# Projection pairs two at a time in program order, and the start of attention inside the last two

## The chip, the core and the metric

The kernel runs on one core of a Trainium2 chip. The metric is device time in microseconds for one launch: 2081.24 us before, the median of 3 runs (2080.03 to 2082.38).

## The reference

One layer of a streaming encoder on a 1024 x 1024 float32 input: a feed-forward block, a combined projection, a gated convolution beside differential attention, an output projection, a second feed-forward block, a final norm.

```python
h = x + 0.5 * swiglu(rms_norm(x, norm_ffn1), ffn1_gate, ffn1_up, ffn1_down)
u = rms_norm(h, norm_mix)
xc, bg, cg, q, k, v, g_conv, g_attn = split(u @ w_in)      # 1024 x 5120
y_conv = (bg * causal_conv3(cg * xc)) @ w_conv_out
q, k = rope(q), rope(k)                                    # 8 half heads of 64
o = softmax(q1 k1^T / 8, chunk mask) @ v - lam * softmax(q2 k2^T / 8, chunk mask) @ v
y_attn = ((1 - lam_init) * rms_norm(o)) @ w_attn_out
h = h + (sigmoid(g_conv + b) * y_conv + sigmoid(g_attn + b) * y_attn) @ w_o
h = h + 0.5 * swiglu(rms_norm(h, norm_ffn2), ...)
out = rms_norm(h, norm_final)
```

## The kernel before

Stages follow one another on one core: feed-forward 1, the projection with `w_in`, attention, the two branches' output projections, `w_o`, feed-forward 2. Each fp32 operand of a large product is split into a high and a low part of a narrower type (`split`, L245: a cast on ScalarE, ACT, for the high part, a subtraction on VectorE, DVE, for the low one), and a product is three matmuls (`mm3`, L264).

The projection has 20 blocks of weights of 1 MB. Sixteen are multiplied before attention and four (the second gate, `g_attn`) during it, as filling for the tensor engine (PE). A block, called a **pair**, is two column blocks of `w_in`: for example `c,0` holds `cg` and `xc` of a quarter of the convolution, `k,0` the two rotary halves of four half heads. Pairs 0 and 1 run as plain jobs; pairs 2 to 15 run by a seven-product scheme in the order `ORDER = (2, 1, 7, 6, 4, 5, 3)` (`pair_jobs`, L279). So a pair is seven **jobs**, and a job is 12 matmuls of 128x512 (L267).

A job has a `prep`, which sums quarters of the weight block on DVE (L243), casts the sum on ACT (L248, tiles `A` and `F`) and subtracts on DVE (L243), and a `run`: the 12 matmuls, then the eviction of the PSUM bank into one of ten `C` buffers, by an ACT copy where the target is new (L308) and a DVE add where it isn't (L310). The seven jobs of a pair share three accumulating chains: job 2 alone, jobs 1, 6, 5, 3, and jobs 7, 4. Job 6 goes on in the bank of job 1 and so must come after that bank has been read out; likewise 5 after 6, 3 after 5, and 4 after 7. `submit` (L214) keeps four jobs ahead: `prep` of job n+4 stands in the program ahead of `run` of job n.

When a pair's results are done, a function for its kind runs at once: `rope_done` (L800; six DVE products and sums and eight stores for each half), `v_done` (L825; a store), `conv_done` (L831; two DVE multiply-adds and an ACT scaling for each half, stored in `zd`), `bg_done` (L856; loads `zd` back, multiplies by the gate, stores `yd`). The pairs go k0, q0, v0, k1, q1, v1, c0, c1, b0, c2, c3, b1 (`PAIRS`, L882) after the first gate's four.

From `k.flush()` (L1260) backward, a scheduler of the framework orders the instructions of each engine by estimates of its own. From L1262 on, `manual_schedule` holds PE, DVE, ACT and GpSimd (POOL) to the order of the program; the queue of DMA issues on SyncE (SP) is scheduled throughout. [...]

In `run`, after the flush, the first steps of `filling` load and split block 16 of `w_in`; `attend` begins with `head(0)` (L901: loads of keys and values of head 0, casts L918, POOL subtractions L919, eight transposes of the values L929 and their splits), between whose steps four filling steps run (`FIRST`, L1241; six matmuls of L1159 each), then `load_q` (L934), then 16 **units** of attention. A score is L955, with a mask matmul L957. Each unit has filling steps of its own; what is left of the filling when the units are done runs after them.

## Time and profile before

| what | us or share |
|---|---|
| median of 3 runs | 2081.24 |
| profiled execution: its own time | 2082.11 |
| profiled execution: span | 2080.3 |
| PE busy | 1981.0 (95%) |
| DVE busy | 1402.0 (67%) |
| ACT busy | 935.1 (45%) |
| POOL busy | 136.8 (7%) |
| pairs 2 to 15, first matmul at 714.15 to last eviction's start at 1013.55 | 299.40 |
| from there to the first score at 1027.88 | 14.33 |
| unit 0 of attention, to 1038.54 | 10.66 |

The stretches are cut by the starts of instructions in the timeline. A matmul's end is modelled, so the pitch of successive jobs tells more than the duration of a row.

### The profile page before, as it was taken

Reading aid. Unit: us, or ns where it says so; the run is one execution under the profiler, and the core shown is the slowest. Engines: PE = TensorE matmul, PEld = TensorE weight load, DVE = VectorE, ACT = ScalarE, POOL = GpSimd, SP = SyncE. Lnnn points to the kernel's source line nnn. Section 1 sums busy time; section 2 is a strip of 40 time slices with the busy share of each in tenths; the row PEclk is TensorE's granted clock in tenths of the full one; section 3 lists DMA queues with packets and bytes.
Section 4 is the critical chain, followed back from the end, with each engine's and each line's share of the span. In section 5 each row is a group of like instructions: output and inputs, shape, how many; then the busy total and the mean of one; then the engine's idle time right before and its main releaser. Section 6 shows DMA issues by size and latency. Waiting matters only on the chain.

```text
span 2080.3 us, 24145 instructions
## 1 busy us (share of the span) xinstructions
PE 1981.0 (95%) x8808; PEld 1624.7 (78%) x8808; DVE 1402.0 (67%) x2166; ACT 935.1 (45%) x1684; POOL 136.8 (7%) x123
## 2 busy tenths in 40 slices
PE   9799999999999999999799997999999999999997
PEld 8588888888877877777578775877788888888885
DVE  8965665676866856656376737798865665666874
ACT  7433333353464633233366656456433333353362
POOL 0000000000000000000244445000000000000000
PEclk9899999999999999999899998999999999999998
DMA  5223223264543423312333344423223223274441
GB/s 213 84 109 113 95 102 117 81 236 159 194 157 111 152 98 100 126 57 71 119 105 122 97 148 144 190 81 132 97 102 121 86 101 112 82 264 152 150 154 59
DMA packets 81208, 259.70 MB, mean 125 GB/s; under 512 B 10048, under 2 KB 16320, under 8 KB 63936
## 3 DMA queue, kind: packets, MB, share of 16 engines
q1 hardware_dynamic: 81088, 258.15, 34.8%
q8 instruction: 69, 1.13, 0.2%
q14 instruction: 51, 0.42, 0.1%
HBM read 183.14 MB, written 74.97 MB: 124 GB/s over the span
## 4 chain that ended last, share of the span: by engine, by line
PE 81%; DVE 10%; ACT 3%; issue 2%; POOL 1%; DMA 1%; SPq 0%; DVEq 0%; ACTq 0%; POOLq 0%
PE sc L267 37%; PE at L267 16%; PE ps L267 9%; PE ot L267 8%; DVE Q L243 3%; PE ps L1159 2%; DVE A L243 1%; DVE C L243 1%; DVE F L243 1%; PE ps L1221 1%; PE sc L955 1%; PE sc L339 1%; PE sc L338 1%; PE sc L337 1%; PE sc L1221 1%
## 5 line engine op out<-in xcount | busy, mean ns | idle before, releaser
L267 PE MATMUL sc<-Q,A 128*128 128x512 f32 x1968 | 473.5, 390 | 2.4 <-ACT C L308 2.4
L267 PEld LDWEIGHTS sc<-Q,A 128*128 128x128 f32 x1968 | 369.7, 188 | 81.3 <-ACT C L308 3.2
L267 PE MATMUL sc<-Q,F 128*128 128x512 f32 x1548 | 382.1, 396 | 29.5 <-ACT Q L248 11.4
L267 PEld LDWEIGHTS sc<-Q,F 128*128 128x128 f32 x1548 | 294.6, 191 | 96.9 <-ACT Q L248 12.9
L243 DVE TENSOR_TENSOR F<-Q,F 128x512 fp32r<-128x512 f32 (+1 forms) x307 | 211.8, 696 | 170.1 <-ACT F L248 169.7
L248 ACT CAST F<-Q 128x512 fp32r<-128x512 f32 (+1 forms) x315 | 190.0, 612 | 256.5 <-PE sc L267 88.1
L243 DVE TENSOR_TENSOR Q<-Q,Q 128x512 fp32r<-128x512 f32 (+4 forms) x334 | 278.7, 887 | 33.6 <-ACT Q L248 26.8
L248 ACT CAST A<-Q 128x512 fp32r<-128x512 f32 (+1 forms) x299 | 180.3, 611 | 268.0 <-PE sc L267 159.1
L243 DVE TENSOR_TENSOR A<-Q,A 128x512 fp32r<-128x512 f32 (+1 forms) x299 | 202.0, 678 | 130.2 <-ACT A L248 129.3
L267 PE MATMUL at<-Q,F 128*128 128x512 f32 x1128 | 279.4, 393 | 10.1 <-ACT C L308 9.2
L267 PEld LDWEIGHTS at<-Q,F 128*128 128x128 f32 x1128 | 213.0, 189 | 57.3 <-ACT C L308 10.9
L248 ACT CAST Q<-Q 128x512 fp32r<-128x512 f32 (+1 forms) x214 | 153.1, 759 | 87.0 <-DVE Q L243 31.1
L243 DVE TENSOR_TENSOR C<-C,C 128x512 f32<-128x512 f32 x236 | 161.5, 688 | 16.6 <-DMA C<-zd 5.0
L243 DVE TENSOR_TENSOR Q<-Q 128x512 f32<-128x512 f32 x216 | 148.3, 690 | 3.7
L267 PE MATMUL ps<-Q,A 128*128 128x512 f32 x498 | 124.2, 390 | 0.0
L308 ACT COPY C<-sc 128x512 f32<-128x512 f32 x88 | 51.4, 588 | 156.5 <-PE sc L267 155.4
L267 PE MATMUL ot<-Q,A 128*128 128x512 f32 x450 | 112.8, 392 | 0.9 <-DVE Q L398 0.9
L267 PEld LDWEIGHTS ps<-Q,A 128*128 128x128 f32 x498 | 93.6, 188 | 19.6 <-issue 0.3
L1159 PE MATMUL ps<-Q,F 128*128 128x512 f32 x384 | 105.9, 412 | 3.1 <-ACT C L1165 3.1
L267 PE MATMUL at<-Q,A 128*128 128x512 f32 x444 | 107.6, 389 | 0.8 <-DVE C L310 0.8
L310 DVE TENSOR_TENSOR C<-C,sc 128x512 f32<-128x512 f32 x81 | 55.6, 687 | 75.3 <-ACT C L308 35.1
L267 PEld LDWEIGHTS ot<-Q,A 128*128 128x128 f32 x450 | 85.3, 190 | 19.0 <-issue 1.3
(218 smaller groups left out, 2190.6 us busy)
## 6 DMA issues: line engine op xcount, KB each, us to landing
Q<-in_ffn_gate SPq DMA_DIRECT2D x21, 1024.0 KB, 5.8
Q<-in_ffn_up SPq DMA_DIRECT2D x21, 1024.0 KB, 4.8
Q<-in_w_in SPq DMA_DIRECT2D x20, 1024.0 KB, 5.4
g1d<-C SPq DMA_DIRECT2D x77, 256.0 KB, 2.0
g2d<-C SPq DMA_DIRECT2D x77, 256.0 KB, 2.0
Q<-in_ffn_down SPq DMA_DIRECT2D x16, 1024.0 KB, 6.5
Q<-g1d SPq DMA_DIRECT2D x14, 1024.0 KB, 6.3
Q<-g2d SPq DMA_DIRECT2D x14, 1024.0 KB, 5.8
```

Source lines behind the costliest of these rows:

```text
L243: e.tensor_tensor(out, a, b, op)
L248: self.nc.scalar.copy(hi, src)
L267: mm = lambda *x, **kw: self.nc.tensor.matmul(*x, skip_group_check=True, **kw)
L308: nc.scalar.copy(C[o, t], ps)
L310: nc.vector.tensor_tensor(C[o, t], C[o, t], ps, ALU.add)
L337: mm(ps, a[:, 0, q], hi[:, q], start=n == q == 0, stop=False)
L338: mm(ps, a[:, 0, q], lo[:, q], start=False, stop=False)
L339: mm(ps, a[:, 1, q], hi[:, q], start=False, stop=n == 1 and q == 3)
L955: nc.tensor.matmul(sc[:, a : a + w], qs[:, hl, s, qb * P : (qb + 1) * P], kst[:, s, a : a + w], start=hl == 0, stop=hl == 1 and a + w < n)
L1159: nc.tensor.matmul(ps, a[kk][:, x, q], y[:, q], start=c == 0, stop=c == 23)
L1221: nc.tensor.matmul(ps, a[:, x, kk], b[:, y, kk % 2], start=c == 0, stop=c == 11)
```

## The change

The pairs 2 to 15 are taken two at a time by `two`, a **couple**: jobs of the two pairs alternate in the program. The order of pairs becomes b0 with k0, b1 with q0, c0 with v0, c1 with k1, c2 with q1, c3 with v1, after the gate's couple (2, 3). Couple (2, 3) is still ordered by the scheduler; the six couples from pair 4 on stand inside `manual_schedule`, so the written order is their order. The rope and convolution work is put into a queue `slow`, from which `aside` takes a step or two after each job. The gate `b` now comes before the convolution: it is stored in `bd`, and the convolution loads it and multiplies. During the last couple the nine steps of `head(0)` are appended to `slow`. After the last job is submitted, `load_q(0, 0)` and the first filling step (load and split of block 16) are issued, then the last jobs run. The four `FIRST` filling steps are no longer run there.

```diff
+    def aside(self, n=None):
+        for _ in range(min(len(self.slow), n or (2 if len(self.slow) > 3 else 1))):
+            self.slow.popleft()()
...
                 if LAST[o, t] == i:
                     done(o, t, C[o, t])
+                self.aside()
...
-        self.zd = [d(f"zd{j}", [P, SEQ]) for j in range(4)]
+        self.bd = [[d(f"bd{a}{t}", [P, 2, TH]) for t in range(2)] for a in range(2)]
...
+            def products():
+                tt(b, x2, sin, ALU.mult)
+                tt(d, x1, sin, ALU.mult)
+                tt(x1, x1, cos, ALU.mult)
+
+            def sums():
+                tt(x2, x2, cos, ALU.mult)
+                tt(x1, x1, b, ALU.subtract)
+                tt(x2, x2, d, ALU.add)
+                for hh, x in ((0, x1), (1, x2)):
+                    for c4 in range(4):
+                        nc.sync.dma_start(dst[c4, 32 * hh : 32 * hh + 32, t * TH : (t + 1) * TH], x[32 * c4 : 32 * c4 + 32, :])
+
+            k.slow.extend((products, sums))
...
+            def half(th):
+                zc, z, b = X[0, th], Z[th], k.C()
+                nc.sync.dma_start(b, self.bd[j // 2][th][:, j % 2])
                 nc.scalar.mul(zc, z[:, 2:], w(2))
...
-                nc.sync.dma_start(self.zd[j][:, th * TH : (th + 1) * TH], zc)
+
+                def gated():
+                    k.tt(zc, zc, b, ALU.mult)
+                    nc.sync.dma_start(self.yd[j // 2][th][:, j % 2], zc)
+
+                k.slow.appendleft(gated)
+
+            k.slow.extend((lambda: half(0), lambda: half(1)))
...
-             + [("k", 0), ("q", 0), ("v", 0), ("k", 1), ("q", 1), ("v", 1)]
-             + [("c", 0), ("c", 1), ("b", 0), ("c", 2), ("c", 3), ("b", 1)]
+             + [("b", 0), ("k", 0), ("b", 1), ("q", 0), ("c", 0), ("v", 0)]
+             + [("c", 1), ("k", 1), ("c", 2), ("q", 1), ("c", 3), ("v", 1)]
...
-            tp = k.ps("at")
+            tp = k.ps("at") if h else k.psd()
...
-        for i, _ in enumerate(self.head(0)):
-            if i in self.FIRST:
-                fill()
-        for _ in self.load_q(*units[0]):
-            pass
+        for _ in self.first:
+            fill()
...
-                if n == 2 and len(raws) < ns:
+                if n in (2, 4) and len(raws) < ns:
                     raws.append(k.load_raw(io["w_in"][len(raws)]))
...
-        for idx in range(2, ns):
-            project(k.pair_jobs(raws[idx], B, self.done(idx)))
-        k.flush()
+        doubles = lambda idx: project(k.two(*(k.pair_jobs(raws[i], B, self.done(i)) for i in (idx, idx + 1))))
+        doubles(2)
         ET = mybir.EngineType
         with k.tc.manual_schedule(engines={ET.PE, ET.DVE, ET.Activation, ET.Pool}):
+            self.first = self.head(0)
+            for idx in range(4, ns, 2):
+                if idx == 4:
+                    self.cs = k.t("Q", [P, 2, SEQ])
+                    nc.sync.dma_start(self.cs, io["rope"])
+                if idx == ns - 2:
+                    k.slow.extend([lambda: next(self.first, None)] * 9)
+                doubles(idx)
...
+            queries = self.load_q(0, 0)
+            next(queries)
             next(fill)
+            k.step()
+            for _ in queries:
+                pass
+            k.flush()
+            while k.slow:
+                k.aside()
```

Two places show it in the queues of the engines. A name such as `C_757_6426` is a buffer's tag and a running number.

**Place 1**, ACT where one pair ends and the next begins, before: `at_739` is here the bank of v1's last job, `at_751` and `ps_756` are banks of the first jobs of the next pair, c0.

```order
L248 CAST A_758_6428<-Q_746_6334 128x512
L308 COPY C_749_6371<-at_739_6267 128x512
L308 COPY C_752_6390<-at_751_6377 128x512
L308 COPY C_757_6426<-ps_756_6413 128x512
L248 CAST A_763_6466<-Q_746_6334 128x512
```

The same engine after, within the couple b1, q0; the four banks hold jobs of the two pairs in turn.

```order
L314 COPY C_694_5872<-at_693_5859 128x512
L254 CAST A_695_5874<-Q_649_5493 128x512
L314 COPY C_697_5890<-sc_696_5877 128x512
L254 CAST F_698_5893<-Q_644_5453 128x512
L314 COPY C_699_5908<-at_689_5822 128x512
L254 CAST A_700_5911<-Q_649_5493 128x512
L314 COPY C_701_5926<-sc_691_5842 128x512
```

Before, three copies stand in a row, and the first of them reads a bank that PE writes later than the other two; after, copies and casts alternate in the order in which PE fills the banks.

**Place 2**, DVE at the end of the last pair, before: `at_836` and `sc_839` are banks of b1's jobs. The low part of block 16's first slice (`F_854`) stands nine rows ahead of this piece.

```order
L310 TENSOR_TENSOR C_834_7081<-C_834_7081,at_836_7087 128x512
L850 SCALAR_TENSOR_TENSOR C_830_7051<-C_831_7053,cst_1_85,C_830_7051 128x512
L243 TENSOR_TENSOR C_834_7081<-C_834_7081,C_837_7101 128x512
L851 SCALAR_TENSOR_TENSOR C_830_7051<-C_831_7053,cst_1_85,C_830_7051 128x512
L310 TENSOR_TENSOR C_841_7135<-C_841_7135,sc_839_7108 128x512
L243 TENSOR_TENSOR C_841_7135<-C_841_7135,C_842_7150 128x512
L310 TENSOR_TENSOR C_840_7121<-C_840_7121,at_836_7087 128x512
```

After, at the end of the last couple (c3, v1): `C_846` takes the eviction of v1's job 4 from `sc_830`; `C_840` and `C_842` take those of the two jobs 5, from `at_834` and `sc_837`; `Q_859` is block 16, `Q_856` an operand of the filling.

```order
L316 TENSOR_TENSOR C_846_7119<-C_846_7119,sc_830_6968 128x512
L256 CAST Q_857_7166<-Q_856_7164 128x512
L249 TENSOR_TENSOR Q_858_7167<-Q_856_7164,Q_857_7166 128x512 x2
L256 CAST Q_857_7166<-Q_856_7164 128x512
L249 TENSOR_TENSOR F_860_7178<-Q_859_7176,F_860_7178 128x512
L316 TENSOR_TENSOR C_840_7052<-C_840_7052,at_834_6995 128x512
L316 TENSOR_TENSOR C_842_7072<-C_842_7072,sc_837_7019 128x512
```

And the DMA queue, SP, there, before and after: the load of block 16 and its neighbours.

```order
L863 DMA yd00_3219<-C_792_6723 128x512
L276 DMA Q_853_7207<-in_w_in 128x2048
L863 DMA yd01_3220<-C_790_6706 128x512
L861 DMA C_800_6787<-zd0_3235 128x512
L863 DMA yd01_3220<-C_799_6785 128x512
```

```order
L956 DMA C_854_7160<-qkq0_3211 64x2x256 x2
L840 DMA vd3_3218<-C_846_7119 128x512
L282 DMA Q_859_7176<-in_w_in 128x2048
L840 DMA vd3_3218<-C_842_7072 128x512
L863 DMA C_864_7231<-bd10_3237 128x512
```

The low part of block 16's first slice now stands on DVE ahead of the evictions of both jobs 5, and the load of block 16 stands on SP behind the store of `C_846`, which waits for the first of these rows; before, it stood among the stores of `yd0`.

## Rows read from the trace of the kernel before

**Rows 1.** The page: busy time per engine; shares of the chain that ended last.

```profile
PE 1981.0 (95%) x8808; PEld 1624.7 (78%) x8808; DVE 1402.0 (67%) x2166; ACT 935.1 (45%) x1684; POOL 136.8 (7%) x123
...
PE 81%; DVE 10%; ACT 3%; issue 2%; POOL 1%; DMA 1%; SPq 0%; DVEq 0%; ACTq 0%; POOLq 0%
```

**Rows 2.** Windows: stretch, length, busy us per engine (count), PE's granted clock, DMA share, GB/s.

```profile
150.00:250.00 100.00, 100.00 (x443) 82.83 (x442) 59.62 (x91) 37.68 (x66) 0.00 (x0) 1.00 0.30 114
714.15:1013.55 299.40, 280.03 (x1195) 226.12 (x1193) 181.90 (x285) 99.22 (x175) 4.58 (x7) 0.98 0.30 99
1013.55:1027.88 14.33, 4.53 (x14) 3.46 (x15) 2.01 (x3) 4.89 (x9) 4.99 (x5) 0.64 0.56 168
1027.88:1038.54 10.66, 9.79 (x36) 8.10 (x37) 3.29 (x9) 6.03 (x17) 4.28 (x4) 0.69 0.43 135
1242.40:1277.70 35.30, 34.21 (x135) 24.78 (x134) 22.10 (x20) 21.63 (x37) 25.57 (x18) 1.00 0.39 119
```

**Rows 3.** Window of the filling line L1159 alone: PE and PEld only.

```profile
714.15:1013.55 299.40, 4.57 (x18) 3.38 (x18) 0.98 0.30 99
```

**Rows 4.** Timeline of PE: start, us, instructions, idle before and its releaser.

```profile
809.46 4.50 PE L267 MATMUL at<-Q,F 128*128 128x512 f32 x12 [2.59 <-ACT C L308]
...
816.51 2.88 PE L267 MATMUL ps<-Q,F 128*128 128x512 f32 x12
819.23 2.88 PE L267 MATMUL sc<-Q,A 128*128 128x512 f32 x12
822.89 3.01 PE L267 MATMUL sc<-Q,F 128*128 128x512 f32 x12 [0.78 <-DVE C L310]
...
895.46 3.01 PE L267 MATMUL ps<-Q,F 128*128 128x512 f32 x12 [1.43 <-ACT C L308]
```

**Rows 5.** Timeline of ACT at the boundary of place 1.

```profile
893.84 1.07 ACT L308 COPY C<-at 128x512 f32<-128x512 f32 x2 [10.03 <-PE at L267]
894.80 0.60 ACT L308 COPY C<-ps 128x512 f32<-128x512 f32 x1
```

**Rows 6.** Timeline of PE from the last projection job to the first score.

```profile
1010.53 3.02 PE L267 MATMUL at<-Q,A 128*128 128x512 f32 x12 [0.78 <-DVE C L310]
1022.07 1.11 PE L929 MATMUL at<-ident,C 128*128 128x128 f32 x4 [8.53 <-DMA C<-vd]
1025.54 1.05 PE L929 MATMUL at<-ident,C 128*128 128x128 f32 x4
1027.88 0.45 PE L955 MATMUL sc<-Q,A 128*128 128x128 f32 x1 [1.29 <-ACT A L943]
```

**Rows 7.** Timeline of DVE in the pairs.

```profile
777.42 1.29 DVE L243 TENSOR_TENSOR C<-C,C 128x512 f32<-128x512 f32 x2
...
939.38 0.74 DVE L851 SCALAR_TENSOR_TENSOR C<-C,cst,C 128x512 f32<-128x512 f32 x1
...
947.32 2.38 DVE L243 TENSOR_TENSOR Q<-Q,Q 128x512 fp32r<-128x512 f32 x2
...
1015.14 0.69 DVE L243 TENSOR_TENSOR C<-C,C 128x512 f32<-128x512 f32 x1 [3.94 <-DMA C<-zd]
```

**Rows 8.** Timeline of POOL beside it.

```profile
946.89 1.66 POOL L243 TENSOR_TENSOR Q<-Q,Q 128x512 fp32r<-128x512 f32 x1 [50.23 <-DVE A L243]
```

**Rows 9.** Timeline of SP: DMA issues.

```profile
951.42 0.33 SPq L276 DMA_DIRECT2D Q<-in_w_in  x1
...
1011.60 0.43 SPq L861 DMA_DIRECT2D C<-zd  x1
```

**Rows 10.** DMA issues between 700 and 1060: count, KB each, median us to landing.

```profile
Q<-in_w_in SPq DMA_DIRECT2D x14, 1024.0 KB, 5.3
```

**Rows 11.** Timeline of PE after a long pause, behind attention.

```profile
1286.42 1.22 PE L1221 MATMUL sc<-Q,F 128*128 128x512 f32 x2 [8.66 <-ACT F L248]
...
1289.94 4.39 PE L1221 MATMUL sc<-Q,F 128*128 128x512 f32 x10 [1.05 <-DVE F L243]
1294.17 2.45 PE L1221 MATMUL ps<-Q,A 128*128 128x512 f32 x10
```

More of the change, by code (lines that the diff above doesn't have):

```diff
@@ L177, in __init__ @@
         self.bg = deque()
+        self.slow = deque()
         self.rot = self.na = 0
@@ L811, in done @@
             tt = k.tt
-            tt(b, x2, sin, ALU.mult)
-            tt(d, x1, sin, ALU.mult)
-            tt(x1, x1, cos, ALU.mult)
-            tt(x2, x2, cos, ALU.mult)
-            tt(x1, x1, b, ALU.subtract)
-            tt(x2, x2, d, ALU.add)
-            dst = self.qk[which, p]
-            for hh, x in ((0, x1), (1, x2)):
-                for c4 in range(4):
-                    nc.sync.dma_start(dst[c4, 32 * hh : 32 * hh + 32, t * TH : (t + 1) * TH], x[32 * c4 : 32 * c4 + 32, :])
+            dst = self.qk[which, p]
+            def products():
[10 more added lines that the diff above has]
+            k.slow.extend((products, sums))
         return done
@@ L846, in done @@
             w = lambda a: k.cst[:, C_CW + 3 * j + a : C_CW + 3 * j + a + 1]
-            for th in range(2):
-                zc, z = X[0, th], Z[th]
+            def half(th):
+                zc, z, b = X[0, th], Z[th], k.C()
+                nc.sync.dma_start(b, self.bd[j // 2][th][:, j % 2])
                 nc.scalar.mul(zc, z[:, 2:], w(2))
@@ L859, in done @@
         def done(o, t, c):
-            zc = k.C()
-            nc.sync.dma_start(zc, self.zd[2 * jp + o][:, t * TH : (t + 1) * TH])
-            k.tt(c, c, zc, ALU.mult)
-            nc.sync.dma_start(self.yd[jp][t][:, o, :], c)
+            nc.sync.dma_start(self.bd[jp][t][:, o, :], c)
         return done
@@ L888, in loads @@
         k = self.k
-        r = [k.load_raw(k.io["w_in"][0]), k.load_raw(k.io["w_in"][1])]
-        self.cs = k.t("Q", [P, 2, SEQ])
-        k.nc.sync.dma_start(self.cs, k.io["rope"])
-        return r
+        return [k.load_raw(k.io["w_in"][0]), k.load_raw(k.io["w_in"][1])]
     def done(self, idx):
@@ L1240 @@
     NPLAIN = 4
-    FIRST = (4, 5, 6, 7)
     def run(self, raws, f, load_h, done, pre):
```

## The prediction

> **What bounds the kernel now.** I read the page first: PE is busy 95% of the span and carries 81% of the chain that ended last, DVE is busy 67% and is 10% of that chain [rows 1]. So time is to be had only where PE stands still or runs at a lower clock, and the windows say where. In feed-forward 1, where two pairs of products alternate in the program, PE is busy the whole of 100 us at a granted clock of 1.00, with DVE busy 60% [rows 2]. In the projection's pairs it isn't: 299.40 us hold 280.03 busy; then come 14.33 us with 4.53 busy at a clock of 0.64, and unit 0 with 0.69 [rows 2].
>
> The timeline shows the pauses. Two jobs start 2.72 us apart (816.51 and 819.23), and that pitch is the price of 12 matmuls when nothing is missing, 0.227 us each [rows 4]. A pair has two kinds of pauses. At its boundary PE waits 1.4 to 2.6 us for an ACT copy; behind the longer ones 12 matmuls take 4.50 us where they otherwise show 2.88, since the clock has fallen. And its last job waits 0.78 us for a DVE eviction, because the chain's bank can't be written on before it has been read [rows 4]. ACT shows the first kind as a queue: at place 1 two copies in a row begin at 893.84, after 10.03 us of waiting for PE's last job of the old pair; the copy of `ps`, behind them, begins at 894.80, and PE, which needs that bank, goes on at 895.46 [rows 5, 4]. The bank of `ps` had been filled long before. So the first kind comes from the order on ACT, the second from a chain with nothing beside it.
>
> The stretch after the pairs is another thing: the last job begins at 1010.53, and PE next works at 1022.07, having waited 8.53 us for the values' load; the first score is at 1027.88 [rows 6].
>
> **The change part by part.**
>
> *The pairs.* 14 pairs x 7 jobs x 2.72 = 266.6 us is the dense time of the work from 714.15 on; its 98 x 12 = 1176 matmuls remain. Of the 299.40 us, 18 are filling matmuls, 18 x 0.227 = 4.1 [rows 3], and 299.4 - 266.6 - 4.1 = 28.7 are pauses and low clock. With two pairs alternating, a job of the other pair (2.72) lies between two jobs of one chain, which covers the 0.78; the ACT copies stand in the order in which the banks fill, which ends the 1.4 to 2.6. What can be late next is DVE. It is busy 181.9 us here [rows 2]; over 266.6 that is 68%, against 60% in feed-forward 1, where two alternating pairs leave no pause. The margin is 32% of a couple's 38.1 us, some 12 us, but the order is now the written one: `aside` puts three rope products (0.65 each from the pair at 777.42, 1.9 together [rows 7]) or two convolution steps (0.74 each) between an eviction and the next job's operands. An eviction has 2.72 us from the end of its job to the start of the next of its chain: its own 0.65 and 1.9 fit, with 0.2 left. I take 0.3 us for each of the seven couples, 2 in all; the bounds are 0 and 8, the latter one pause of about 1.2 per couple.
>
> *Head 0.* The 14.33 us from 1013.55 to the first score go. Their loads, casts, and POOL subtractions come to lie beside the last couple's matmuls. Eight transposes stay on PE's path, 1.11 + 1.05 as shown; by then the values' load may be just late. I take 1.7, bounds 0.8 to 3. Six filling matmuls in that stretch move away too.
>
> *The load of block 16.* Here the change adds a wait. On SP it stands behind the store of `C_846`, which waits for the DVE eviction of v1's job 4; on DVE the low part of its first slice stands ahead of the evictions of both jobs 5, and PE's last two jobs wait for those. From the end of job 4: eviction 0.65, the store's issue 0.43 [rows 9], the load 5.3 [rows 10], a cast 0.6, the low part 0.65, the eviction of job 5 0.65, and some 0.5 for hand-overs (0.06 between the end of the copy at 895.40 and PE at 895.46, several times over): 8.8. In that time PE has two jobs, 5.4. So the third stands still for 3.4 us; bounds 1.5 (a load without neighbours) and 8 (a load that shares the DMA engines with the last rope stores and head 0's loads). Before, the load was issued at 951.42, far from any end [rows 9], and cost nothing. Then the clock: after a pause of 2.59 twelve matmuls take 1.6 more, after one of 8.66 the next fourteen take (1286.42 to 1294.17) 7.75 instead of 3.2, of which 1.05 is a pause [rows 4, 11]. For 3.4 I take 2.0, nearer the first; bounds 0 and 4.
>
> Up to the first score: 266.6 + 2.0 + 1.7 + 3.4 + 2.0 = 275.7 in place of 299.4 + 14.3 = 313.7, a gain of 38.0.
>
> *Unit 0.* It took 10.66 us at a clock of 0.69 with 36 matmuls, 9.79 busy [rows 2]; at full clock some 3 us less. But its first maxima stand on DVE behind the last convolution steps, six operations of 0.65 to 0.74 (4.2 us), which nothing covers but the first score. I take 0, bounds -3 and +3.
>
> *The filling.* Four steps of six matmuls, 24, no longer run ahead of attention; the units have their own, so 24 remain for its end. There PE is busy 34.21 of 35.30 at a clock of 1.00 [rows 2], so they cost 24 x 0.227 = 5.4; the lower bound is 0, if the pauses behind that stretch (8.66 [rows 11]) take them up.
>
> *POOL.* Eight subtractions now fall in the last couple. At 946.89 one took 1.66 beside two DVE subtractions of 2.38, which take 1.29 together without it [rows 7, 8]: 1.1 of DVE's time. With DVE's margin of 12 us even eight such (8.8) fit; I take 0, and the bound is one of them in front of an eviction, 1.1. [...]
>
> The sum: -38.0 + 0 + 5.4 = -32.6. The profiled execution took 2082.1, 0.9 over the median of 2081.2 and well inside what three runs spread, so 2082.1 - 32.6 = **2049.5**.
>
> **The rivals.**
>
> (a) *Slower: the written order on DVE and ACT.* Both execute in order, and a scheduler's order is replaced by one that knows no durations. The place is DVE within each of the six written couples: a convolution product that waits for the load of the gate, as DVE waited 3.94 us at 1015.14 for `zd` [rows 7], holds every operand and eviction behind it. Two such waits in a couple are 8 us, and the clock falls after each (1.6). The decision point is 32.6 / 6 = 5.4 us lost per couple; at two waits with their clock, 11 x 6 = 67 less 2 already counted, the time would be 2114, at 8 us per couple 2096. For it: every `C` buffer is needed, 10 for about 16 tiles a couple, so that loads are issued late. Against: the gate's product is a step of its own, taken a job or more after its load was issued, and the load issued at 1011.60 served the product at 1015.14, 3.5 us or 1.3 jobs later [rows 7, 9]. [...]
>
> (b) *Faster, but with half of it eaten.* The same mechanism in two or three couples only, or buffers late for the operands: 10 to 27 us back, 2066 to 2077.
>
> (c) *No change.* Pauses of the first kind return in full as DVE pauses: 28.7 of the 38.0 back, with the filling's 5.4: 2078 to 2085.
>
> (d) *The larger gain.* Block 16 lands in time (-5.4), the filling disappears in later pauses (-5.4) and unit 0 gains its clock (-3): 2036, with DVE's 2 also 2034; beyond that there is nothing to take.
>
> That it doesn't do what it says is excluded: the queues of place 1 show the new order, and head 0's steps stand among the last couple's jobs.
>
> **How the numbers follow.** The forecast with its bounds covers 2034 (all at the lower end) to 2066 (stalls in order +6, block 16 +4.6, clock +2, unit 0 +3, rounded): 0.76. Case (b) 0.10, (c) within 0.2% 0.04, (a) 0.07, below 2034 0.03. 0.2%, 4 us, is about what a measurement of this kernel can tell from no change. That makes faster 0.89, same 0.04, slower 0.07. The range holds the forecast and the nearer end of (b): 2034 to 2068.
>
> **What would show it.** In the profile after: from the first job of couple (2, 3) to the last projection job 266 to 275 us; no ACT copy ahead of which ACT waits 10 us; the load of block 16 issued within some 10 us of the last job, one pause of 2 to 5 us on PE behind it, released by DVE, and a clock below 1 after it; the first score near 990; more L1159 matmuls or later work after the last unit. I am wrong if PE shows pauses in every couple with DVE as releaser (a), if the pause at block 16 is missing or over 8, or if the gain up to the first score is there and lost again in the units.

## The result, and the profile after

The changed kernel takes 2047.38 us (2045.84 to 2049.32, 4 runs) against 2080.95 for the kernel before in the same comparison: a ratio of 0.9839, 95% interval 0.9822 to 0.9856. The forecast was 2049.5, a gain of 32.6 in the profiled execution; that gained 35.5 (2082.11 to 2046.62). The total fits better than its parts do: too little was charged up to the first score, and stretches that were put at nothing made up for most of it.

| stretch | before | after | gain | forecast gain |
|---|---|---|---|---|
| up to the first matmul of pair 2 | 714.15 | 713.33 | 0.8 | 0 |
| from there to the first score | 313.73 | 281.30 | 32.4 | 38.0 |
| unit 0 | 10.66 | 9.54 | 1.1 | 0 |
| unit 1 to the long pause | 239.23 | 242.60 | -3.4 | -5.4 |
| the long pause | 8.65 | 8.76 | -0.1 | 0 |
| from its end to the end of the span | 793.88 | 788.97 | 4.9 | 0 |

The windows of the profile after, cut at the same events (stretch, length, busy us of PE, PEld, DVE, ACT and POOL with their counts, granted clock, DMA share, GB/s), answer to [rows 2]:

```profile
713.33:947.73 234.40, 231.93 (x1021) 191.16 (x1020) 151.47 (x237) 86.55 (x155) 5.21 (x7) 1.00 0.31 105
947.73:994.63 46.90, 40.96 (x164) 33.55 (x165) 31.39 (x48) 14.98 (x27) 5.82 (x6) 0.89 0.37 116
994.63:1004.17 9.54, 7.15 (x38) 5.79 (x36) 5.14 (x12) 5.75 (x16) 1.52 (x2) 1.00 0.34 110
1004.17:1246.77 242.60, 228.24 (x1221) 187.34 (x1219) 151.85 (x281) 152.84 (x373) 116.80 (x97) 1.00 0.37 117
1255.53:2044.50 788.97, 764.11 (x3332) 627.40 (x3332) 551.92 (x826) 343.40 (x570) 1.29 (x1) 0.99 0.35 129
```

The same two last stretches of the kernel before, from its own windows:

```profile
1038.54:1277.77 239.23, 224.42 (x1197) 184.99 (x1195) 148.53 (x276) 149.89 (x367) 115.88 (x96) 0.99 0.36 113
1286.42:2080.30 793.88, 767.28 (x3332) 628.90 (x3332) 553.96 (x828) 343.64 (x571) 0.92 (x1) 0.98 0.35 129
```

The pairs are dense: 85 jobs at 2.72 are 231.2, and PE goes from 713.33 to 945.38 (947.73 less a wait of 2.35), 232.05, at a clock of 1.00. What is left of pauses stands at the end of the last couple. The timeline of PE there (start, us, instructions, idle before and its releaser; an L273 is the L267 of before, L945 the transposes, L971 a score):

```profile
947.73 0.98 PE L945 MATMUL sc<-ident,C 128*128 128x128 f32 x4 [2.35 <-DMA C<-vd]
...
949.22 3.96 PE L273 MATMUL sc<-Q,A 128*128 128x512 f32 x12
953.01 2.88 PE L273 MATMUL at<-Q,F 128*128 128x512 f32 x12
...
974.77 2.88 PE L273 MATMUL at<-Q,F 128*128 128x512 f32 x12
977.49 2.88 PE L273 MATMUL sc<-Q,A 128*128 128x512 f32 x12
986.31 5.46 PE L273 MATMUL at<-Q,F 128*128 128x512 f32 x12 [5.94 <-DVE C L316]
...
994.63 0.33 PE L971 MATMUL sc<-Q,A 128*128 128x128 f32 x2
```

The window of the last two jobs, behind the pause, has a granted clock of 0.64:

```profile
986.31:994.63 8.32, 8.32 (x24) 6.62 (x25) 2.62 (x5) 1.21 (x2) 1.69 (x3) 0.64 0.36 111
```

So the 281.30 us are 266.6 of jobs, 0.85 spread over the dense couples, 2.35 of waiting for the values, 1.5 of transposes (947.73 to 949.22), 1.1 of low clock in the job behind (3.79 to the next start, not 2.72; the clock there is 0.73), 5.94 of pause ahead of the last two jobs, and 2.9 of clock in these (994.63 - 986.31 = 8.32, not 5.44): 281.2.

The pause is the place foreseen, seen on DVE (L316 is an eviction, L249 a subtraction, sum or product, L256 a cast) and on SP:

```profile
975.02 0.68 DVE L316 TENSOR_TENSOR C<-C,ps 128x512 f32<-128x512 f32 x1
975.74 1.66 DVE L249 TENSOR_TENSOR C<-C,C 128x512 f32<-128x512 f32 x1
977.32 0.68 DVE L249 TENSOR_TENSOR A<-Q,A 128x512 fp32r<-128x512 f32 x1
977.92 0.68 DVE L316 TENSOR_TENSOR C<-C,sc 128x512 f32<-128x512 f32 x1
...
984.87 0.69 DVE L249 TENSOR_TENSOR F<-Q,F 128x512 fp32r<-128x512 f32 x1 [4.28 <-ACT F L254]
985.48 0.68 DVE L316 TENSOR_TENSOR C<-C,at 128x512 f32<-128x512 f32 x1
```

```profile
937.74 3.59 SPq L832 DMA_DIRECT2D qkq<-C  x8
941.38 2.37 SPq L929 DMA_DIRECT2D C<-qkk  x4
943.85 1.00 SPq L940 DMA_DIRECT2D C<-vd  x2
...
978.62 0.34 SPq L840 DMA_DIRECT2D vd<-C  x1
979.06 0.38 SPq L282 DMA_DIRECT2D Q<-in_w_in  x1
```

The eviction of v1's job 4 starts at 977.92; its store is issued at 978.62, block 16's load at 979.06; the low part starts at 984.87, the eviction of job 5 at 985.48, PE goes on at 986.31. That chain is 8.4 us from the eviction's start, as worked out (8.8). But the eviction itself was 3.1 us late: job 4 had ended when the next one began, at 974.77. In these 3.15 us DVE finished a low part (0.25), evicted job 4 of c3, which had ended at 972.05 (0.72), formed the product of c3's convolution (the row of 1.66; 1.58 to the next start) and subtracted the next job's low part (0.60). Ahead of that it had waited three times for an ACT cast (0.69, 0.69 and 0.31, between 970.7 and 974.4), since in the written order a job's low part stands right behind the sum that ACT has to cast first. Between 752 and 980 DVE has 26 such waits of about 0.69 (0.68 to 0.74); four of them end between 958 and 980, where the scheduler's order, below, has none of that length.

The first three rows of SP tell of the values: their loads are issued at 943.85, behind eight rope stores (3.6 us of issuing) and four loads of keys (2.4).

Part of this is scatter. In three kernels below whose edits take effect only behind this place (split behind, load ahead, filling ahead) the wait for the values is 1.64 to 1.70 us, and wait, transposes and clock together cost 2.7 to 2.8, not 4.9; in a fourth (operand behind) they cost 5.2. The row of the first:

```profile
946.28 0.63 PE L945 MATMUL sc<-ident,C 128*128 128x128 f32 x4 [1.70 <-DMA C<-vd]
```

### The profile page after: what moved, and what is told of

It is laid out like the page before. It is cut to its first block, busy times and chain, and to the rows that moved or that the text cites. A ratio compares the mean times of both kernels' runs of the same rounds, so it can differ in the third digit from the quotient of the medians.

```text
span 2044.5 us, 24147 instructions
## 1 busy us (share of the span) xinstructions
PE 1967.0 (96%) x8808; PEld 1617.8 (79%) x8808; DVE 1404.5 (69%) x2166; ACT 934.2 (46%) x1684; POOL 137.2 (7%) x123
## 4 chain that ended last, share of the span: by engine, by line
PE 40%; DVE 6%; ACT 2%; issue 2%; DMA 1%; POOL 1%; SPq 0%; POOLq 0%; DVEq 0%; ACTq 0%
PE sc L273 16%; PE at L273 7%; PE ps L273 4%; PE ot L273 3%; PE ps L1172 2%; DVE Q L249 2%; PE sc L1234 1%; PE sc L971 1%; PE ot L1047 1%; DMA C<-in_w_conv_out 1%; DVE F L249 1%; DVE sm L982 1%; PE ps L1234 1%; DVE Q L1005 1%; PE at L1017 0%
## 5 line engine op out<-in xcount | busy, mean ns | idle before, releaser
L273 PE MATMUL sc<-Q,A 128*128 128x512 f32 x2052 | 494.6, 391 | 1.7 <-ACT C L314 1.7
L273 PEld LDWEIGHTS sc<-Q,A 128*128 128x128 f32 x2052 | 386.2, 188 | 84.0 <-ACT C L314 2.1
L273 PE MATMUL sc<-Q,F 128*128 128x512 f32 x1464 | 360.0, 395 | 23.5 <-ACT Q L254 9.7
L273 PEld LDWEIGHTS sc<-Q,F 128*128 128x128 f32 x1464 | 278.5, 191 | 85.3 <-ACT Q L254 10.8
L249 DVE TENSOR_TENSOR F<-Q,F 128x512 fp32r<-128x512 f32 (+1 forms) x307 | 213.0, 698 | 175.0 <-ACT F L254 174.7
L249 DVE TENSOR_TENSOR Q<-Q,Q 128x512 fp32r<-128x512 f32 (+4 forms) x334 | 276.9, 878 | 33.2 <-ACT Q L254 25.7
L273 PE MATMUL at<-Q,F 128*128 128x512 f32 x1164 | 286.4, 392 | 7.3 <-DVE C L316 5.9
L249 DVE TENSOR_TENSOR A<-Q,A 128x512 fp32r<-128x512 f32 (+1 forms) x299 | 203.5, 682 | 128.4 <-ACT A L254 127.9
L273 PEld LDWEIGHTS at<-Q,F 128*128 128x128 f32 x1164 | 219.8, 189 | 54.6 <-ACT A L959 6.3
L249 DVE TENSOR_TENSOR C<-C,C 128x512 f32<-128x512 f32 x236 | 162.3, 691 | 18.4 <-ACT C L314 9.2
L249 DVE TENSOR_TENSOR Q<-Q 128x512 f32<-128x512 f32 x216 | 148.6, 692 | 2.3
L273 PE MATMUL ps<-Q,A 128*128 128x512 f32 x474 | 118.2, 390 | 0.0
L1172 PE MATMUL ps<-Q,F 128*128 128x512 f32 x384 | 103.0, 403 | 4.3 <-ACT C L1178 4.2
L273 PE MATMUL ot<-Q,A 128*128 128x512 f32 x426 | 106.8, 391 | 0.0
L273 PEld LDWEIGHTS ps<-Q,A 128*128 128x128 f32 x474 | 89.1, 188 | 18.5 <-ACT A L254 0.2
L273 PE MATMUL ps<-Q,F 128*128 128x512 f32 x420 | 101.5, 389 | 0.0
L273 PE MATMUL at<-Q,A 128*128 128x512 f32 x408 | 98.9, 390 | 0.0
L273 PEld LDWEIGHTS ot<-Q,A 128*128 128x128 f32 x426 | 80.5, 189 | 16.9 <-ACT A L254 0.2
```

The source lines that it names most:

```text
L249: e.tensor_tensor(out, a, b, op)
L273: mm = lambda *x, **kw: self.nc.tensor.matmul(*x, skip_group_check=True, **kw)
L1172: nc.tensor.matmul(ps, a[kk][:, x, q], y[:, q], start=c == 0, stop=c == 23)
```

## The experiments

Each kernel is the changed one (2047.4) with the edit shown, unless another is named; each was timed against the kernel before in the same comparison.

| kernel | us | ratio to before (95%) | first score at | from there to the end of the long pause | rest |
|---|---|---|---|---|---|
| changed | 2047.38 | 0.9839 (0.9822 to 0.9856) | 994.63 | 260.9 | 789.0 |
| pairs in turn | 2069.67 | 0.9942 (0.9927 to 0.9956) | 1024.02 | 258.2 | 788.8 |
| scheduler's order | 2035.07 | 0.9773 (0.9759 to 0.9788) | 983.76 | 262.2 | 788.6 |
| head 0 behind | 2054.02 | 0.9857 (0.9840 to 0.9873) | 1002.91 | 257.2 | 793.2 |
| split behind | 2043.71 | 0.9817 (0.9802 to 0.9831) | 985.74 | 267.0 | 791.4 |
| load ahead | 2040.29 | 0.9803 (0.9788 to 0.9818) | 986.20 | 261.7 | 789.9 |
| values later | 2046.97 | 0.9832 (0.9817 to 0.9847) | 992.46 | 261.8 | 790.8 |
| filling ahead | 2051.34 | 0.9858 (0.9841 to 0.9876) | 1000.27 | 255.1 | 794.7 |
| scheduler, values later | 2042.54 | 0.9807 (0.9789 to 0.9826) | 983.11 | 266.0 | 793.1 |
| operand behind | 2045.21 | 0.9819 (0.9803 to 0.9835) | 987.37 | 265.9 | 791.8 |
| couples alone | 2050.32 | 0.9846 (0.9831 to 0.9860) | 997.81 | 254.4 | 792.7 |

The last three columns are from the profiled execution of each, the first one in the span's own time, "rest" up to the span's end. The four executions of one kernel lie 2 to 6 us apart, and the profiled one can be up to 3.5 from the median (couples alone: 2046.81), so differences of a few us are read from the stretches.

### Does alternation do it, or the written order?

```diff
-                doubles(idx)
+                in_turn(idx)      # all seven jobs of one pair, then of the other
```

> The six couples from pair 4 on run as pairs one after the other (all seven jobs of the first, then all seven of the second); still in written order, everything else as in the changed kernel (2047.4). Theory A, two pairs alternating is what removes the pauses: jobs 5 and 3 of a pair stand side by side again, so each of the 12 pairs pays at least the 0.78 us eviction wait of before, and 1 to 2 us where a rope or convolution step lies ahead of the eviction on DVE, some with a lower clock behind: 10 to 25 us more, 2057 to 2072. Theory B, the written order of ACT's copies is what removed them and alternation adds nothing: within 4 us of 2047.

Measured 2069.67, 22 more: theory A. PE's timeline has thirteen pauses released by a DVE eviction, of 0.62 to 2.93 us, and one of 5.12 released by an ACT copy; here the first and the longest:

```profile
769.05 3.01 PE L273 MATMUL sc<-Q,F 128*128 128x512 f32 x12 [0.78 <-DVE C L316]
...
1014.91 5.49 PE L273 MATMUL ps<-Q,F 128*128 128x512 f32 x12 [5.12 <-ACT C L314]
```

The 0.78 is that of before, to the hundredth [rows 4]; the 1.4 to 2.6 for an ACT copy of before is gone except at the end, and longer waits for DVE have come. So the written order did end the waits of place 1, but by itself it doesn't cover the chain; alternation does.

```diff
-        with k.tc.manual_schedule(engines={ET.PE, ET.DVE, ET.Activation, ET.Pool}):
-            self.first = self.head(0)
-            for idx in range(4, ns, 2):
+        self.first = self.head(0)
+        for idx in range(4, ns, 2):
...
+        with k.tc.manual_schedule(engines={ET.PE, ET.DVE, ET.Activation, ET.Pool}):
```

> All seven couples alternate as in the changed kernel, with head 0 among the last couple's jobs, but the scheduler orders the engines until the last job is submitted; only what follows stands in written order. Theory A, alternation does it and a scheduler's order would do as well: PE without pauses in the couples, 2043 to 2052. Theory C, the written order is needed, since the scheduler again puts an ACT copy that waits ahead of ready ones: 1.4 to 2.6 us at some couple boundaries, 2053 to 2065.

Measured 2035.07: 12.3 less than the changed kernel and lower than either theory gave. PE's timeline from the last couple to unit 0 has no pause ahead of the last two jobs:

```profile
952.86 0.63 PE L945 MATMUL sc<-ident,C 128*128 128x128 f32 x4 [1.46 <-DMA C<-vd]
...
978.32 2.88 PE L273 MATMUL at<-Q,F 128*128 128x512 f32 x12
...
983.76 0.33 PE L971 MATMUL sc<-Q,A 128*128 128x128 f32 x2
```

SP shows one reason: the load of block 16 has been put between the rope stores, 15.7 us earlier than in the changed kernel, ahead of the store of v1's sum.

```profile
963.40 0.37 SPq L282 DMA_DIRECT2D Q<-in_w_in  x1
...
973.87 5.71 SPq L840 DMA_DIRECT2D vd<-C  x2
```

That isn't all, for the kernel with the load ahead, below, still has a pause of 3.24 us. DVE shows the other reason: the casts and subtractions that stand between the last evictions in the changed kernel run from 962.4 to 966.7 here, and ahead of the eviction of job 4 it is DVE that waits for PE:

```profile
973.15 0.69 DVE L316 TENSOR_TENSOR C<-C,sc 128x512 f32<-128x512 f32 x1 [0.18 <-PE sc L273]
```

The profiled executions are 10.3 us apart, and the first score comes 10.9 earlier (994.63 to 983.76); 8.8 of these are the pause for block 16 and its clock. Theory C, that a scheduler brings back the waits of place 1, is refuted: with two pairs in the program it finds ready work.

```diff
-            if idx == ns - 2:
-                k.slow.extend([lambda: next(self.first, None)] * 9)
...
+        k.flush()        # then, as before: head 0 with FIRST filling steps, load_q
```

> The alternation alone: couples in the scheduler's order as in the fastest kernel so far (2035.1), with the deferred rope and convolution steps, but head 0, the four filling steps and the first load of queries behind the last job, as in the kernel before. Theory A, the 28.7 us of pauses in the pairs are worth 28.7 by themselves and head 0's place is worth what is left: 2081.5 - 28.7 = 2053 (2050 to 2057). Rival, with the pairs dense the loads of head 0 come no earlier and wait longer: 2058 to 2062. Rival, alternation and head 0 overlap in what they save: under 2048.

Measured 2050.32, the near edge of what theory A gave. From the first job to the start of the last, 97 jobs and 11 filling matmuls, PE is busy the whole time at a clock of 1.00:

```profile
713.20:979.53 266.33, 266.33 (x1176) 220.53 (x1175) 176.46 (x281) 99.41 (x174) 4.44 (x7) 1.00 0.32 106
```

Later PE waits 8.44 us for the values, as it did 8.53 before [rows 6]. So in the scheduler's order the couples, with their deferred steps and the new order of pairs, are worth about 32 us (0.9846) without head 0's place, and that place is worth 15 more by the medians, 10.5 by the profiled executions. Alternation without the deferred steps and with the old order of pairs wasn't run; the pairs in turn keep both and lose 22, so they aren't enough without it.

### Head 0

```diff
-                if idx == ns - 2:
-                    k.slow.extend([lambda: next(self.first, None)] * 9)
...
-        for _ in self.first:
-            fill()
+        for i, _ in enumerate(self.first):
+            if i in (4, 5, 6, 7):
+                fill()
```

> The nine steps of head 0 and the four filling steps between them come after the last job, as in the kernel before; couples as in the changed kernel. Theory A, head 0's loads were worth their 14.3 us of stretch less the 4.9 that the changed kernel still pays for them (2.35 of waiting, 1.5 of transposes, 1.1 of clock): +9.4, less 3.5 for the 24 filling matmuls that leave the end of attention: 2053 (2050 to 2058). Rival, head 0's place is worth little since the pause for block 16 covers its loads: 2045 to 2049.

Measured 2054.02, 6.6 more: theory A. The wait for the values is 7.65 us there, and the first score comes 8.3 us later. In the scheduler's order head 0's place brings the first score 14.1 us forward (997.81 to 983.76). Of the difference, 3.7 are the pause for block 16 with its clock, which costs 8.8 in the changed kernel and 5.2 here (3.45 of pause at 979.68, 1.7 of clock).

### Block 16

```diff
+        raw[todo[0][0]] = k.load_raw(k.io["w_in"][todo[0][0]])
+        yield                                   # and a second next(fill) ahead of attend
         ws = weights(*todo[0])
```

> The load of block 16 stays where it is; the casts and subtractions of its first slice stand behind the last jobs' evictions and the last convolution steps, ahead of attention. Theory A, PE's pause ahead of its last two projection jobs (5.94 us, and 2.9 of low clock behind it) comes from the order on DVE, where the slice's low part waits for the load ahead of the eviction of job 5: it goes, 2047.4 - 8.8 = 2038.6 (2036 to 2042). Rival, the load is late for whoever needs it and the pause moves to the first filling step in unit 0: 2044 to 2049.

Measured 2043.71, between the two. PE's timeline:

```profile
980.21 2.97 PE L273 MATMUL at<-Q,F 128*128 128x512 f32 x12 [2.69 <-DVE C L316]
...
987.71 0.73 PE L1174 MATMUL ps<-Q,F 128*128 128x512 f32 x2 [1.55 <-ACT F L254]
991.04 2.07 PE L1174 MATMUL ps<-Q,F 128*128 128x512 f32 x4 [2.61 <-DVE F L249]
```

The pause ahead of the last two jobs fell from 5.94 to 2.69, and of its 2.9 of clock 0.1 is left. The first score came 8.9 us earlier: 6.0 by that, and 2.9 because PE was further along already behind the transposes, which the edit doesn't touch. But the first filling step (L1174) waited 1.55 and 2.61 for block 16's slices, and the stretch behind the first score grew by 6.1. So the order on DVE and the late load each have a share; moving the need is not enough.

```diff
                     k.slow.extend([lambda: next(self.first, None)] * 9)
+                    k.slow.append(lambda: setattr(self, "early", k.load_raw(io["w_in"][ns])))
...
-        raw = {}
+        raw = {todo[0][0]: self.early}
```

> The changed kernel with one thing moved: the load of block 16 is put among the steps of the last couple, behind head 0's, so that on SP it stands ahead of the store of v1's sum and of the rope stores; its casts and subtractions stay in their places. Theory A, the pause of 5.94 us is the load's place on SP (the load ends 5 us after the eviction that its issue waits for), and a part of some 2.7 us is DVE being late with the eviction of job 4 and of job 5 (as the pause that is left when the split stands behind them, 2.69, shows): 5.94 becomes 2.7 to 3.4, the clock behind it 2.9 becomes about 0.5, unit 0 as before: 2047.4 - 5.5 = 2042 (2040 to 2044). Rival, DVE's lateness was itself made by the load: no pause, 2038 to 2039. Rival, another wait takes its place: 2046 to 2049.

Measured 2040.29, 7.1 less, inside what theory A gave. The load is issued at 960.90. The pause falls to 3.24 and the clock behind it costs 0.1, together 5.5 less, as worked out; the first score comes 8.4 earlier, and the other 2.9 are again gained up to the transposes, ahead of the edit. The pause that is left, and DVE ahead of it:

```profile
980.66 2.99 PE L273 MATMUL at<-Q,F 128*128 128x512 f32 x12 [3.24 <-DVE C L316]
```

```profile
976.64 0.67 DVE L316 TENSOR_TENSOR C<-C,sc 128x512 f32<-128x512 f32 x1
977.23 0.41 DVE L256 CAST Q<-Q 128x512 fp32r<-128x512 f32 x1
977.68 1.29 DVE L249 TENSOR_TENSOR Q<-Q,Q 128x512 fp32r<-128x512 f32 x2
978.89 0.42 DVE L256 CAST Q<-Q 128x512 fp32r<-128x512 f32 x1
979.23 0.69 DVE L249 TENSOR_TENSOR F<-Q,F 128x512 fp32r<-128x512 f32 x1
979.83 0.68 DVE L316 TENSOR_TENSOR C<-C,at 128x512 f32<-128x512 f32 x1
```

In these rows DVE isn't waiting for anything; it is late by its own work, and by the same three waits for ACT casts ahead of them (1.69 us, up to 973.1).

```diff
-            for c in range(4):
-                k.split(u[:, c], hi[:, c], lo[:, c], 0.7, 0.5, "pl")
...
+        yield                                   # behind the last convolution steps
+        for c in range(4):
+            k.split(u[:, c], hi[:, c], lo[:, c], 0.7, 0.5, "pl")
```

This edit is made on top of the load ahead.

> The kernel with block 16's load ahead (2040.3) with one thing more: the casts and subtractions of the filling's other operand (ud), of which two casts and two subtractions run on DVE between the evictions of jobs 4 and 5, stand behind the last convolution steps. Theory A, the pause of 3.24 us that is left ahead of PE's last two jobs is DVE's lateness: 2.0 of it those four operations, 1.2 the backlog of rope sums that makes the eviction of job 4 start at 976.64 in place of some 974.7. So the pause becomes about 1.2 and the first score comes 2 us earlier; in unit 0 the four operations (2.1) delay the first maxima, so the whole is about the same: 2038 to 2041. Rival, the pause is set by something else and stays at 3.2: 2040 to 2043.

```profile
981.80 3.01 PE L273 MATMUL at<-Q,F 128*128 128x512 f32 x12 [0.88 <-DVE C L316]
...
996.25 0.80 PE L971 MATMUL sc<-Q,A 128*128 128x256 f32 x2 [5.30 <-ACT Q L989]
```

The pause fell to 0.88, as theory A had it: it was DVE's work. The time, 2045.21, is out of what was expected: the same operations in front of the first softmax raised the wait in unit 0 from 2.39 to 5.30, 2.9 where 2.1 had been worked out, and the transposes came 1.9 us later than in the kernel it was built on, which lies ahead of the edit and is scatter like that told of above.

### The values, and the filling

```diff
         yield
+        for _ in range(2 if h == 0 else 0):
+            yield
         for a, vraw in enumerate(vraws):
```

> The changed kernel with two empty steps between the loads of head 0's values and their transposes, which so come one job later on PE. Theory A, the wait of 2.35 us for the values and the 1.1 us of clock behind it go, all else stays: 2044 (2042 to 2046). Rival, the pause for block 16 grows by as much, since its eviction hangs on DVE's backlog and not on PE: 2046 to 2049.

Measured 2046.97, in the rival's range, and 0.4 from the changed kernel. The wait for the values goes, a wait of 1.55 for an ACT copy comes in its place, and the pause at block 16 is longer than in the changed kernel:

```profile
946.34 3.04 PE L273 MATMUL sc<-Q,A 128*128 128x512 f32 x12 [1.55 <-ACT C L314]
...
984.79 5.11 PE L273 MATMUL at<-Q,F 128*128 128x512 f32 x12 [7.32 <-DVE C L316]
```

ACT shows where the 1.55 is from: a cast of head 0's keys waits for its load, which stands on SP behind the rope stores, and a cast and the copy of a job (945.70) stand behind it.

```profile
944.66 0.62 ACT L934 CAST Q<-C 128x512 fp32r<-128x512 f32 x1 [4.65 <-DMA C<-qkk]
```

The changed kernel has that wait too (4.41 us, to 944.74); there PE waits longer still for the values, which hides it. The mechanism isn't settled by this kernel: its first score comes 2.2 us earlier, so not all of the gain is lost at block 16, and the two stretches behind, which the edit doesn't touch, take the rest back (0.9 and 1.8). Nor is the longer pause surely the edit's, since the kernel with the filling ahead, below, has one of 7.79 with nothing changed ahead of it.

The same two steps in the scheduler's kernel:

> The scheduler's order for all couples (2035.1) with the two empty steps ahead of the values' transposes. Theory A, the wait of 1.46 us for the values goes and nothing comes in its place: 2033 to 2034. Rival, the scheduler moves other work by as much: 2035 to 2037.

Measured 2042.54, 7.5 worse, which neither theory gave. The wait for the values fell to 0.77 and the first score came 0.65 us earlier, but the stretch behind it grew by 3.8 (the first wait in unit 0 is 3.60, not 2.39), and the rest by 4.5. Why the units are slower isn't settled.

```diff
-        for _ in self.first:
+        for _ in range(4):
             fill()
```

> The changed kernel with four filling steps (24 matmuls) put back ahead of the first score. Theory A, they cost 5.4 us there and give 3.5 to 5.4 back at the end of attention, where they no longer stand: 2047 to 2050. Rival, the filling is free wherever it stands behind attention: 5.4 more, 2052 to 2054. Rival, ahead of the first score they cover the last convolution steps on DVE, so that unit 0 loses its wait of 2.39: 2044 to 2046.

Measured 2051.34, 4 more, between what theory A and the first rival gave. Ahead of the first score the 24 matmuls take the 5.4 us that they were put at (994.83 to 1000.27). The windows from the first score to the long pause, of this kernel and then of the changed one, differ by the 24 matmuls (1233 and 1257):

```profile
1000.27:1246.74 246.47, 231.31 (x1233) 189.78 (x1231) 151.35 (x283) 155.92 (x384) 118.72 (x98) 0.99 0.37 116
```

```profile
994.63:1246.77 252.14, 235.39 (x1257) 193.14 (x1255) 156.99 (x292) 158.59 (x389) 118.32 (x98) 1.00 0.37 117
```

That is 5.7 us less, but not by the matmuls alone: unit 0 takes 7.86 us here and not 9.54, because its wait of 2.39 is gone, as the second rival had it. The 24 matmuls at the end account for the other 4.0. The first score comes 5.6 later, so the two cancel, and the loss lies in the rest (794.7 against 789.0), which is told of below. This kernel also shows how far two profiles of the same order can differ: nothing ahead of the first score is edited but the filling itself, and the pause for block 16 is 1.85 longer than in the changed kernel.

```profile
987.31 4.95 PE L273 MATMUL at<-Q,F 128*128 128x512 f32 x12 [7.79 <-DVE C L316]
```

## Why the prediction was right, point by point

**The pairs** (266.6 + 2.0): right, and shown. Couples run at the pitch of 2.72 with 0.85 us lost where 2 were allowed. That alternation does it is shown by the pairs in turn (+22) and by the couples alone (-32, where 28.7 were worked out). One of the signs named for it failed, though: four ACT copies in the couples start after 10.20 us of waiting, with no pause on PE behind them; the first:

```profile
786.97 0.59 ACT L314 COPY C<-at 128x512 f32<-128x512 f32 x1 [10.20 <-PE at L273]
```

So a long wait on ACT was no harm in itself; at place 1 (10.03 us) it was one because PE needed a bank whose copy stood behind it and waited 1.43 us [rows 4, 5]. Two other signs were missed at the end of the last couple: its last job starts 278.2 us after the first job of couple (2, 3), not 266 to 275, and the pause is over 5.

**Rival (a), the written order**: its condition was put in the wrong place. It loses next to nothing in the couples, where 5.4 us each would have decided; it loses 12.3 us against the scheduler's order, most of it at the end of the last couple. Two of its mechanisms are in the traces: the low part that waits 4.28 us for the load ahead of ready evictions, and the key cast that waits 4.41 (4.65 in the kernel with values later). That DVE and ACT hold ready work behind a waiting row is shown by these: the banks of the two jobs 5 had been filled by about 980.2, and their evictions started at 985.48 and 986.08, behind the low part at 984.87; the copy of a job whose bank had been filled by 942.5 started at 945.78, behind the key cast at 944.74. In case (b) a sum is off: 10 to 27 us back from 2049.5 begin at 2060, not at 2066.

**Head 0** (1.7 for the transposes, bounds 0.8 to 3): mis-sized, 4.9 in this profile (2.35 wait, 1.5 transposes, 1.1 clock), though the three kernels with 2.7 to 2.8 for the same order stay within the bound. The prediction named a load "just late" but didn't count what is ahead of it on SP: eight stores and four loads, 6.0 us of issuing.

**Block 16** (3.4, and 2.0 of clock): the mechanism, its place and its chain were right, and the load ahead, which takes 5.5 us off at this place, shows it. The size was 5.94 and 2.9. The step that failed is "from the end of job 4: eviction 0.65": it took DVE to be free at that moment, by a mean share of 68% over the couples. It was 3.1 us late, behind the other pair's eviction, a convolution product that took 1.66 where POOL was busy, and the next job's low part; the six rope operations had ended at 970.1. 3.4 + 3.1 less 0.4 of a shorter chain is 6.1. The two kernels behind it show the shares: with the load early 3.24 remain, and with the other operand's four operations away 0.88.

**POOL** (0, bound 1.1): one subtraction did meet the eviction's queue, and the DVE product at 975.74 takes 1.66 where 0.69 is usual: 1.0 of the 3.1 us.

```profile
975.55 1.29 POOL L249 TENSOR_TENSOR Q<-Q,Q 128x512 fp32r<-128x512 f32 x1 [27.12 <-ACT Q L254]
```

In the trace POOL's subtraction ends at 976.84 and the product 0.56 us later, at 977.40. The kernel with the operand behind is the test: its edit puts this subtraction behind the last convolution steps, and the same product takes 0.69 us there (at 976.40). The low part behind it takes 1.78 in that kernel (at 977.01) and 0.68 in the changed one; what POOL did beside it there isn't shown. So the product lost 1.0 us beside the subtraction; by what mechanism isn't shown. The bound of 1.1, not the value taken, was the fitting one. The four subtractions of head 0 (POOL at 929.72, 933.79, 945.49 and 946.95) met DVE operations too, which took 1.82, 1.78, 1.39 and 1.75 us (at 929.74, 934.13, 945.91 and 947.23), and ahead of 945 PE's jobs started late by 0.3 us twice (936.66 and 939.66) and no more.

**Unit 0** (0, -3 to +3): -1.1. The clock is 1.00 instead of 0.69, and PE waits 2.39 us for the softmax behind the last convolution steps; both halves were named. What wasn't named is that ACT loads a table in that chain, 1.28 us between the first maxima and the first exponential:

```profile
1000.60 0.50 PE L971 MATMUL sc<-Q,A 128*128 128x256 f32 x2 [2.39 <-ACT Q L989]
```

```profile
998.79 1.28 ACT L989 ACT_TABLE_LOAD   x1
```

**The filling** (5.4): 3.4 between the profiles of before and after, and 4.0 behind unit 0 where only the filling differs; so the term was too large by 1.4 to 2. The clock is 0.99 in the two windows with fewer matmuls and 1.00 in the other; whether that is the difference isn't shown.

**The rest** (0): 4.9 gained, and nothing in the change accounts for it. The stretch's matmuls are the same. A window of 50 us in it, where DVE is the busy engine, before and after:

```profile
1336.42:1386.42 50.00, 44.62 (x185) 35.02 (x184) 50.00 (x77) 22.96 (x41) 0.00 (x0) 0.97 0.17 64
```

```profile
1305.53:1355.53 50.00, 45.48 (x196) 35.77 (x195) 50.00 (x77) 21.87 (x40) 0.00 (x0) 1.00 0.16 64
```

In the kernels of this study the stretch took 788.6 to 794.7 us, with clocks of 0.91 to 1.00 in its first four windows of 50 us. Where this second window has 1.00 (changed, pairs in turn, scheduler's order, load ahead, values later) the stretch took 788.6 to 790.8, where it has 0.97 (before, head 0 behind, split behind, filling ahead, the scheduler with values later), 791.4 to 794.7; whether the clock makes the delay or follows from it isn't shown. Since the stretch is the same code in all of them, the 4.9 are luck. The forecast was 5.6 too high for the gain up to the first score, and that luck, with the 2 of the filling and the 1.1 of unit 0, more than covers it: the errors cancel.

## What to carry to other kernels

When a queue is late, look at what it waits for, then at what stands behind the waiting instruction on every queue: the load of block 16 cost 5.5 us, by what its move took off there, not for its 5.2 us from issue to its first cast (979.06 to 984.22) alone but because its issue waited for an eviction and two evictions waited for its result. A mean busy share doesn't tell whether an engine is free at one moment (DVE was busy 67% from 713.33 to 980.20, and 3.1 us late with one eviction); sum what is queued ahead of that instruction. And where two independent chains are in the program, a scheduler may already find the dense order (here 12.3 us ahead of the written one): before writing an order out by hand, time the alternation alone. And compare two kernels first where their queues are the same: what differs there is scatter (2.7 to 5.2 us at the values here), and an edit that stands behind it has no claim to it.

## What the runs showed of the hardware

Stages whose instructions don't change from kernel to kernel didn't take the same time: 788.6 to 794.7 us behind the long pause, while the granted clock in its first four 50-us windows lay between 0.91 and 1.00. The wait for the values and what follows it cost 2.7 to 5.2 us in kernels whose order up to there is the same. That is as much as many of the edits here, so a comparison of two such kernels under some 5 us should be read stretch by stretch. And short pauses have a second price: behind the pause of 5.94 the two jobs took 2.9 us more (at a clock of 0.64), behind that of 7.79 2.1, behind that of 2.69 or 3.24 about 0.1 (2.97 and 2.99 us for the next job), behind the 2.35 in front of the transposes 1.1 (at 0.73), behind the 3.45 that the kernel with head 0 behind has ahead of the last two jobs 1.7, and behind the 2.59 of the kernel before [rows 4] one job took 1.6 more (at 0.63). The length of the pause alone doesn't tell it.
